# A hybrid mixer layer on one core: the squares of weight blocks kept near their written place on ScalarE, and another order at the output's end

## The chip, the cores and the metric

The kernel runs on one core of one Trainium2 chip. The metric is the device time of one execution in microseconds. A core has five engines with an instruction queue each: TensorE (PE, matmuls; its weight loads are shown as PEld), VectorE (DVE), ScalarE (ACT), GpSimd (POOL) and SyncE (SP), which here only issues DMA transfers. ScalarE and GpSimd issue some transfers too.

## The reference

One layer of a flow-matching backbone, for two groups of tokens, 2048 sample tokens and 128 prompt tokens, with weights shared between them:

```python
xn = rmsnorm(h, ln_g) * (1.0 + scale) + shift          # shift, scale, gate from the conditioning
proj = xn @ w_in                                       # 1024 -> 7696 columns, split by branch
o_a = delta_bidir(...)  * silu(z_a)                    # A: gated delta rule, both directions
o_b = chunk_sgu(u_b, v_b, ...) * silu(z_b)             # B: spatial gating in chunks of 128
o_c = fourier_mix(x_c, grid) * silu(z_c)               # C: real part of an FFT over the grid
merged = sum_n sigmoid(gates[n]) * (o_n @ w_branch[n]) # three branches, 512 -> 1024
h = h + gate * (merged @ w_out)                        # 1024 -> 1024
y = rmsnorm(h, final_g)
```

The outputs are y for the prompt, y for the sample, and the final states of the prompt's delta rule. Everything is in float32; the kernel makes each float32 product of three fp16 matmuls, from a high and a low half of both operands.

## The kernel before, in words

**Stages.** The normalized input is held transposed as fp16 halves (xh, xl: 128 partitions, 8 blocks of 128 channels, 2176 tokens). Tokens are taken in blocks of 512, the last (the prompt) of 128 (TBS). In order of time the kernel computes the silu of z_a, the delta branch's q, k and v (to 440 us in the profile), the spatial gating (to about 745), the Fourier branch (to about 1030), three merges (branch B from about 1030, then C, then A to about 1980), and the output projection with the residual and the last norm (to the end). Since about 440 the delta branch runs beside this as a generator: `pace.tick` and `pace.part` take steps of it by the TensorE time that has been written, first preparation (prep, base_inverse), then from about 890 the scan over chunks, which is a long serial chain of small matmuls.

**Weight blocks.** The input projection and the branch projections are cut into blocks of 128 columns. `read_w` (L291, through `load`) loads a block into a staging buffer `wst`; there are two of these. `converting` (L301 to L328) turns it into halves in steps, each ended by a `yield`: the square (L315, on ScalarE, which writes its squares to the block's low half `lo` as scrap and sums them into `ss`); then a cast of the sum on VectorE (L264), a one-column matmul that adds it over the partitions (`scales`), and a few one-column VectorE instructions for a power-of-two scale; then the high half on ScalarE (L327) and the low half on VectorE (L328), which frees the staging buffer. Large blocks are 128x1024 (`wlo`, `whi`), branch blocks 128x512 (`blo`, `bhi`). `weight_step` takes one such step; `getw(2, 2)` takes the next two blocks and lets the two behind them be converted while these two are used.

In the Fourier stage a loop over four column groups calls `pace.tick` after each part of the work, and every tick takes one weight step. In `merge` (L1699 for the halves of a branch, L1733 for the gate's sigmoid, L1742 and L1743 for the product and the sum) each of eight output blocks goes over five token blocks; behind the gate's and the branch's products of one token block stand a `weight_step()` and a `pace.tick`, so two weight steps. The square of the next gate block is therefore written in the first token block and its one-column matmul directly behind it; the high half and the square of the next branch block are written in the second. At the join of Fourier and the first merge, `branch_block` loads the gated branch from DRAM (`st<-br`, L1689) and makes its halves `big` (o16).

**What sets the order.** The program is written in one order and the Tile scheduler reorders it at compile time: on each engine it issues what it expects to be ready first, with the written order as priority. `tc.issue_after(x)` puts an edge to x on each instruction of a block that goes to x's engine: not before x in the queue, without a wait on the chip. `_InTurn` wraps an engine: with `kept` set, its instructions stay in written order (so at the end of the output: `in_order(True)` for VectorE, ScalarE and TensorE, not for GpSimd); its method `queued()` gives an edge to the engine's newest instruction. `behind_gate()` ties squares and halves to the latest gate sigmoid, but only from the end of the second merge on. Until then a square may be issued as soon as its load is expected.

**The output's end.** The output runs over eight pairs of 128-token row blocks. For the last pair `two_tiles(..., end=True)` and then `prompt_right` write by hand the last products (Y, Z and the prompt's two), the gated residual sums (`add_gated`), the squares for the norm in two or three parts (`squared`), their sums (`summed_up`), the root on GpSimd (`root`), the product with the final gain (`final`), the scaling by the norm (`scaled`) and the stores.

Of the kernel before, what the change touches and what calls it, by code (L numbers as in the profile page):

```python
# [2 lines left out]

# [1 line left out]

# [9 lines left out]
AF = mybir.ActivationFunctionType  # L15
ALU = mybir.AluOpType
# [4 lines left out]
P = 128  # L21
D = 1024
# [7 lines left out]
EPS = 1e-6  # L30
# [138 lines left out]
class _InTurn:  # L169
# [14 lines left out]

        return call

    def queued(self):

        e = self.engine.engine
        newest = next((i for i in reversed(self.tc.nc.cur_bb.bb.instructions) if i.engine == e), None)  # L190
        return ExitStack() if newest is None else self.tc.issue_after(newest)


# [1 line left out]
def hybrid_flow_kernel(ctx: ExitStack, tc: tile.TileContext, x_prompt, x_sample, state_delta, c, c_ctx, w_ada,  # L195
                       b_ada, w_blk, w_bd, a_log, dt_bias, w_spatial, b_spatial, w_brb, w_outb, final_g, w_adb, cols, x_t, x_tp,
                       consts, consts16, y_prompt, y_sample, new_state, dbg=None):
    nc = tc.nc
    SY = nc.sync
    G, V, A, PE = [_InTurn(tc, e_) for e_ in (nc.gpsimd, nc.vector, nc.scalar, nc.tensor)]  # L200
# [17 lines left out]
    ps_mm = pool(ctx, "ps_mm", 3, space=PSUM)  # L218
# [22 lines left out]
    mhalf = sb(cp, [P, 1], "mhalf")  # L241
    G.memset(mhalf, -0.5)

    newest, gated_, queued = [None], [None], [False]

    def behind_gate():
        return tc.issue_after(gated_[0].ins) if queued[0] else ExitStack()
# [55 lines left out]
    def converting(w, st, nkt, cols=P, hi=None, lo=None, tag="w", bufs=5, nth=0):  # L303

        wpool = bwp[0] if tag == "b" else wp
        if tag == "z":
            hi, lo = [sb(p0p, [P, nkt, cols], n_, F16, bufs=4) for n_ in ("zhi", "zlo")]
        if tag == "v":
            hi, lo = [t[:, vfilled[0]] for t in v4]
            vfilled[0] += 1  # L310
        w.hi = sb(wpool, [P, nkt, cols], tag + "hi", F16, bufs=bufs) if hi is None else hi
        w.lo = sb(wpool, [P, nkt, cols], tag + "lo", F16, bufs=bufs) if lo is None else lo
        ss = sb(wp, [P, 1], "wss", bufs=4) if nth < KT else bsums[:, 3 + nth:4 + nth]
        with behind_gate():
            w.squared = A.activation(w.lo, st, AF.Square, accum_out=ss)  # L315
# [11 lines left out]
        w.made = A.activation(w.hi, st, AF.Copy, scale=s)  # L327
        w.low = V.scalar_tensor_tensor(w.lo, st, s, w.hi, ALU.mult, ALU.subtract)  # L328
# [602 lines left out]
    for ct in range(12):  # L931
        w = getw(1, 2 if ct < 6 else min(4, 15 - ct))
        for half in range(1):
# [545 lines left out]
    ps = bank(ps_x, [P, 4, P])  # L1479
# [27 lines left out]
    for t in range(NCH):  # L1507
        ps = bank(ps_mm, [P, 4, P])
# [34 lines left out]
    for g in range(4):  # L1543
# [14 lines left out]
    vst.close()  # L1558


    fs = ExitStack()
    fp = pool(fs, "fp", 1)
    for n_, (a, b) in _COFF.items():
# [14 lines left out]
    for g in range(4):  # L1578
        xw, zw = getw(2, 2)
        for gh in range(1):  # L1580
# [68 lines left out]
            for q4 in range(5):  # L1649
# [8 lines left out]
                if q4 == 2:  # L1658
                    ps = bank(ps_x, [P, P])
# [129 lines left out]
    gates = gate_rows()  # L1789
    s1_, inv_ = branch_scale(1, 20)  # L1790
    inv_ = merge(1, True, inv_, then=(2, 20))
    def finish_delta(db):
        if db == KT - 1:
            pace.drain()
            queued[0] = True
# [97 lines left out]
    ps = bank(ps_x, [P, 27])  # L1893
# [13 lines left out]
    p16, gp, last_load = [], [], []  # L1907
# [36 lines left out]
    wo = _W()  # L1944
# [33 lines left out]
    nth = [0]  # L1978
# [31 lines left out]
    def two_tiles(t, pa, xr, hh, end):  # L2010
# [47 lines left out]
        product(Y, pa, 2, summed(3), False)  # L2058
        Z = bank(ps_mm, [P, 512])
        product(Z, pa, 6, quarter(4, 512), True)  # L2060
        final(hh[0], hh[0], left, left, V)
        final(hh[1], hh[1], right, right, G)
        summed_up(1, 0)
        summed_up(0, 0)
        add_gated(hh[1][:, left], Y, gb[:, left], p1, V)
        squared(1, 1, xr[1], hh[1], left)
        final(hh[1], hh[1], left, left, G)
        add_gated(hh[0][:, right], Z, gb[:, right], u2, V)
        squared(0, 1, xr[0], hh[0], right)
# [7 lines left out]
    def scaled(j, t):  # L2077
        h = last_rows[j]
        A.activation(h, h, AF.Copy, scale=norms[:, j:j + 1])
        SY.dma_start(y_sample[0, (t + j) * P:(t + j + 1) * P], h)  # L2080

    def in_order(kept):
        V.kept = A.kept = PE.kept = kept
# [1 line left out]
    last_rows = []  # L2085
# [3 lines left out]
    def squared(j, i, junk, h, cs):  # L2089
        A.activation(junk[:, cs], h[:, cs], AF.Square, accum_out=parts[j][:, i:i + 1])  # L2090

    def final(out, h, cs, fs, on):
        on.tensor_tensor(out[:, cs], h[:, cs], fg[:, fs], ALU.mult)

    def summed_up(j, i):
        q_ = parts[j]
        if i:
            V.scalar_tensor_tensor(q_[:, i:i + 1], q_[:, i:i + 1], 1.0 / D, q_[:, i - 1:i], ALU.mult, ALU.add)
        else:
            V.tensor_scalar(q_[:, 0:1], q_[:, 0:1], 1.0 / D, EPS, ALU.mult, ALU.add)  # L2100

    def root(j, i):
        G.tensor_tensor(norms[:, j:j + 1], parts[j][:, i:i + 1], mhalf, ALU.pow)
# [12 lines left out]

    def prompt_right():
        cols = slice(0, 384), slice(384, 512)
        summed_up(2, 0)
        for i, cs in enumerate(cols):  # L2120
            ps = bank(ps_mm, [P, cs.stop - cs.start])
            gemm_N(ps, *p16, wo, 512 + cs.start, cs.stop - cs.start)
            add_gated(gp_right[:, cs], ps, gp_right[:, cs], x_right[:, cs], V)
            squared(2, 1 + i, x_right, gp_right, cs)
        scaled(0, firsts[-1])
        f_ = room[:, (2 - 2 * nth[0]) * D:(2 - 2 * nth[0]) * D + 512]
        for cs in cols:
# [7 lines left out]
        SY.dma_start(y_prompt[0, :, right], f_)  # L2135

    in_turn(x_left, xp_[0:P, left])
    next_pair(in_turn)
# [52 lines left out]
```

## Time and profile before

| | us |
|---|---|
| median of three runs | 2145.2 |
| the runs | 2149.37, 2145.2, 2144.76 |
| profiled execution | 2150.07 |
| its span, from the first to the last instruction | 2148.3 |
| TensorE busy in the span | 2085.2 |
| DMA | 403.25 MB, mean 188 GB/s |

The profiled execution is one of its own, 4.87 us above the median of the runs. Times of instructions are counted from the start of its span. A row of a timeline gives start, duration, engine, line, operation and tiles, and in brackets how long the engine was idle before and what released it; x12 is twelve instructions drawn together. A row of the squares and halves reads `wlo<-wst` for a large block and `blo<-wst` for a branch block. In a row of windows stand the stretch, its length, the busy time of PE, PEld, DVE, ACT and POOL with their instructions, the granted TensorE clock as a share of full speed, the DMA engines' busy share and GB/s. In the rows of the output's end, L182 is the wrapper's own line, since instructions in kept order are recorded there.

### The profile page before, as it was taken

The page shows a single profiled execution, that of the slowest core. Times are in us where ns is not written, and L with a number is a line of the kernel's source. Part 1 is how long each engine was busy: PE and PEld are TensorE (multiplying, and loading weights), DVE is VectorE, ACT ScalarE, POOL GpSimd, SP SyncE. Part 2 cuts the span into 40 slices and gives each one's busy share as a digit, 9 for nine tenths or more (in the row PEclk, how much of TensorE's full clock was granted, in tenths as well). Part 3 has the DMA queues.
Part 4 walks back from the last instruction along what each step waited for, and adds up shares of the span by engine and source line. Part 5 has one row for each costly group of instructions (what it writes and reads, how often), then busy time and mean ns, then how long its engine had stood idle before and what let it go on. Part 6 is the DMA issues. An engine that isn't in the chain of part 4 may idle for free.

```text
span 2148.3 us, 42630 instructions
## 1 busy us (share of the span) xinstructions
PE 2085.2 (97%) x16133; PEld 1196.8 (56%) x16133; DVE 1327.9 (62%) x2945; ACT 1060.8 (49%) x2457; POOL 843.3 (39%) x1089
## 2 busy tenths in 40 slices
PE   7999999999999999989899999999999999999997
PEld 4454444455555677777555556565655444444443
DVE  6656854388777786456655555766665564666245
ACT  5554744475656664445544445665653353453112
POOL 0321332225565555542321233354542234333464
PEclk9999999999999999999999999999999999999999
DMA  9525722277877743444655555867664655456852
GB/s 353 219 77 189 267 102 102 74 223 226 259 228 246 225 138 93 121 132 138 205 182 161 167 162 184 258 206 232 210 204 127 209 167 173 167 198 240 335 220 89
DMA packets 222910, 403.25 MB, mean 188 GB/s; under 512 B 39720, under 2 KB 109632, under 8 KB 219888
## 3 DMA queue, kind: packets, MB, share of 16 engines
q1 hardware_dynamic: 167664, 290.84, 42.5%
q0 software_dynamic: 15216, 65.89, 8.2%
q10 hardware_dynamic: 39824, 43.79, 6.0%
q8 instruction: 127, 2.08, 0.4%
q14 instruction: 79, 0.65, 0.1%
HBM read 258.19 MB, written 142.24 MB: 186 GB/s over the span
## 4 chain that ended last, share of the span: by engine, by line
PE 70%; DVE 9%; DMA 9%; ACT 4%; POOL 4%; issue 3%; SPq 1%; ACTq 0%; DVEq 0%; POOLq 0%
PE b L250 66%; PE b L182 4%; DMA st<-br 2%; POOL E L1115 1%; DMA pa<-pa 1%; DMA wst<-in_w_blk_dram 1%; DVE XB L1114 1%; POOL st L1466 1%; DMA ab<-in_w_adb_dram 1%; PE b L1016 1%; DMA sqk<-qk 1%; DMA ei<-XB 0%; ACT xh L182 0%; ACT nd L1066 0%; DVE XB L1123 0%
## 5 line engine op out<-in xcount | busy, mean ns | idle before, releaser
L250 PE MATMUL b<-xh,whi 128*128 128x512 f16 (+1 forms) x1920 | 651.1, 348 | 2.8 <-DVE sg L1456 1.8
L250 PE MATMUL b<-xl,whi 128*128 128x512 f16 (+1 forms) x1920 | 651.2, 348 | 0.0
L250 PE MATMUL b<-xh,wlo 128*128 128x512 f16 (+1 forms) x1920 | 650.1, 347 | 0.0
L250 PEld LDWEIGHTS <-whi 128*128 128x128 f16 x3856 | 352.7, 98 | 326.4 <-issue 7.3
L250 PEld LDWEIGHTS <-wlo 128*128 128x128 f16 x1928 | 188.8, 98 | 176.1 <-issue 2.2
L250 PE MATMUL b<-big,bhi 128*128 128x512 f16 (+1 forms) x960 | 252.3, 347 | 1.9 <-ACT big L1699 1.1
L250 PE MATMUL b<-big,blo 128*128 128x512 f16 (+1 forms) x480 | 163.1, 347 | 0.0
L1743 POOL TENSOR_TENSOR mrow<-mrow,sg 128x512 f32<-128x512 f32 (+1 forms) x80 | 94.4, 1182 | 131.2 <-DVE sg L1742 99.5
L953 POOL TENSOR_TENSOR cy<-cy,raw 128x545 f32<-128x545 f32 (+1 forms) x48 | 65.8, 1395 | 181.8 <-ACT raw L952 181.8
L250 PEld LDWEIGHTS <-xh 128*128 128x128 f16 x1496 | 116.9, 98 | 28.8 <-issue 1.4
L250 PEld LDWEIGHTS <-bhi 128*128 128x128 f16 x960 | 87.7, 98 | 78.1 <-issue 2.6
L1115 POOL TENSOR_TENSOR E<-E,XB 128x31 f32<-128x31 f32 (+15 forms) x155 | 94.1, 607 | 85.7 <-DVE XB L1114 68.8
L250 PEld LDWEIGHTS <-xl 128*128 128x128 f16 x1068 | 98.1, 98 | 44.8 <-DMA tw<-tw 1.4
L1733 ACT ACTIVATE sg<-b,winv 128x512 f32<-128x512 f32 (+1 forms) x120 | 73.9, 616 | 87.1 <-PE b L250 86.4
L1188 POOL COPY T<-ES 32x256 f16<-32x256 f16 x68 | 31.8, 467 | 188.6 <-DMA ES<-ei 167.9
L250 PE MATMUL b<-whi,xh 128*128 128x128 f16 x544 | 92.8, 219 | 0.0
L250 PE MATMUL b<-whi,xl 128*128 128x128 f16 x544 | 92.8, 219 | 0.0
L250 PE MATMUL b<-wlo,xh 128*128 128x128 f16 x544 | 92.8, 219 | 0.0
L328 DVE SCALAR_TENSOR_TENSOR wlo<-wst,wsc,whi 128x1024 f16<-128x1024 f32 x52 | 71.1, 1368 | 33.1 <-ACT whi L327 32.7
L315 ACT ACTIVATE wlo<-wst 128x1024 f16<-128x1024 f32 x52 | 54.9, 1055 | 54.5 <-DMA wst<-in_w_blk_dram 51.2
L1114 DVE TENSOR_TENSOR XB<-XB,E 128x31 f32<-128x31 f32 (+15 forms) x155 | 55.2, 356 | 41.8 <-POOL E L1115 41.2
L1295 POOL TENSOR_TENSOR skn<-skn,ed 128x512 f32<-128x512 f32 x34 | 37.7, 1109 | 109.7 <-DMA skn<-kv 109.7
(532 smaller groups left out, 4317.9 us busy)
## 6 DMA issues: line engine op xcount, KB each, us to landing
wst<-in_w_blk_dram SPq DMA_DIRECT2D x58, 512.0 KB, 4.5
pa<-pa POOLq DMA_DIRECT2D x16, 896.0 KB, 4.4
qkv<-cy POOLq DMA_DIRECT2D x12, 1089.0 KB, 5.3
st<-br SPq DMA_DIRECT2D x48, 256.0 KB, 3.2
mrow<-mrg SPq DMA_DIRECT2D x16, 576.0 KB, 4.6
pa<-pa SPq DMA_DIRECT2D x5, 1792.0 KB, 17.3
dc<-dec SPq DMA_DIRECT2D x17, 512.0 KB, 4.8
kq<-qkv SPq DMA_DIRECT2D x34, 256.0 KB, 4.5
```

Source lines behind the costliest of these rows:

```text
L182: self.last = f(*args, **kw)
L250: newest[0] = PE.matmul(out, l, r, start=start, stop=stop, skip_group_check=reopened)
L315: w.squared = A.activation(w.lo, st, AF.Square, accum_out=ss)
L328: w.low = V.scalar_tensor_tensor(w.lo, st, s, w.hi, ALU.mult, ALU.subtract)
L953: G.tensor_tensor(y[:, c0:c1], y[:, c0:c1], raw[:, 1 + c0:1 + c1], ALU.mult)
L1016: PE.transpose(ps[:, hs(h)], cur[part][:, h, :], ident)
L1114: V.tensor_tensor(t3, X3[:, 0:k, k:k + 1].to_broadcast([P, k, n_]), E3[:, k:k + 1, k:32].to_broadcast([P, k, n_]), ALU.mult)
L1115: G.tensor_tensor(E3[:, 0:k, k:32], E3[:, 0:k, k:32], t3, ALU.subtract)
L1188: G.tensor_copy(T16[rows(a0, b), :, :, b], ES[0:32, :, 2 * a0 + b, :, wT])
L1295: G.tensor_tensor(h3(kn_), h3(kn_), bc(ed[:, d, t, :], P), ALU.mult)
L1733: gated_[0] = A.activation(sg, ps, AF.Sigmoid, scale=gw.inv)
L1743: G.tensor_tensor(mr, mr, sg, ALU.add)
```

## The change

Two edits. First, `queued` takes a number n and gives an edge to the n-th newest instruction of its engine; while the list `scanning` is not empty, from the start of the Fourier stage to the end of the first merge, a weight block's square has an edge to the twelfth newest ScalarE instruction written so far. Loads, halves and sums are not touched.

Second, the hand-written end. VectorE's product of row block 0's left half with the gain (`final(hh[0], left)`) and the first small sums move behind the two last gated sums; GpSimd's left half of row block 1 is written last, and VectorE keeps the right half of row block 0, now in `prompt_right`. The small sums are turned round: the first adds D times epsilon, and only the last multiplies by 1/D. `prompt_right` writes both of its products first, weaves row block 0's sums and root into its own, and lets ScalarE do the prompt's squares before it scales row block 1 and then row block 0. Row block 0's store goes through ScalarE's queue. The prompt's output is put together in one 128x1024 buffer by VectorE, where ScalarE had scaled the left half, and leaves in one store of 512 KB instead of two of 256 KB.

```diff
-    def queued(self):
+    def queued(self, n=1):
         e = self.engine.engine
-        newest = next((i for i in reversed(self.tc.nc.cur_bb.bb.instructions) if i.engine == e), None)
+        own = (i for i in reversed(self.tc.nc.cur_bb.bb.instructions) if i.engine == e)
+        newest = next(islice(own, n - 1, None), None)
         return ExitStack() if newest is None else self.tc.issue_after(newest)
...
-        with behind_gate():
+        with behind_gate(), A.queued(12) if scanning else ExitStack():
             w.squared = A.activation(w.lo, st, AF.Square, accum_out=ss)
...
+    scanning.append(True)
     fs = ExitStack()
...
     inv_ = merge(1, True, inv_, then=(2, 20))
+    scanning.clear()
...
-        final(hh[0], hh[0], left, left, V)
-        final(hh[1], hh[1], right, right, G)
-        summed_up(1, 0)
-        summed_up(0, 0)
         add_gated(hh[1][:, left], Y, gb[:, left], p1, V)
         squared(1, 1, xr[1], hh[1], left)
-        final(hh[1], hh[1], left, left, G)
+        final(hh[1], hh[1], right, right, G)
         add_gated(hh[0][:, right], Z, gb[:, right], u2, V)
         squared(0, 1, xr[0], hh[0], right)
-        summed_up(1, 1)
+        final(hh[0], hh[0], left, left, V)
+        summed_up(1, 0)
+        summed_up(1, 1, True)
         root(1, 1)
-        final(hh[0], hh[0], right, right, V)
-        summed_up(0, 1)
-        root(0, 1)
-        scaled(1, t)
+        final(hh[1], hh[1], left, left, G)
...
-        summed_up(2, 0)
-        for i, cs in enumerate(cols):
-            ps = bank(ps_mm, [P, cs.stop - cs.start])
-            gemm_N(ps, *p16, wo, 512 + cs.start, cs.stop - cs.start)
-            add_gated(gp_right[:, cs], ps, gp_right[:, cs], x_right[:, cs], V)
-            squared(2, 1 + i, x_right, gp_right, cs)
-        scaled(0, firsts[-1])
-        f_ = room[:, (2 - 2 * nth[0]) * D:(2 - 2 * nth[0]) * D + 512]
-        for cs in cols:
-            final(f_, gp_right, cs, slice(512 + cs.start, 512 + cs.stop), V)
+        end = []
+        for cs in cols:
+            end.append(bank(ps_mm, [P, cs.stop - cs.start]))
+            gemm_N(end[-1], *p16, wo, 512 + cs.start, cs.stop - cs.start)
+        V.tensor_tensor(gp_right[:, cols[0]], end[0], gp_right[:, cols[0]], ALU.mult)
+        summed_up(0, 0)
+        summed_up(0, 1, True)
+        root(0, 1)
+        V.tensor_tensor(gp_right[:, cols[0]], gp_right[:, cols[0]], x_right[:, cols[0]], ALU.add)
+        squared(2, 1, x_right, gp_right, cols[0])
+        add_gated(gp_right[:, cols[1]], end[1], gp_right[:, cols[1]], x_right[:, cols[1]], V)
+        squared(2, 2, x_right, gp_right, cols[1])
+        scaled(1, firsts[-1], SY)
+        final(last_rows[0], last_rows[0], right, right, V)
+        summed_up(2, 0)
         summed_up(2, 1)
-        summed_up(2, 2)
+        summed_up(2, 2, True)
         root(2, 2)
-        A.activation(x_left, x_left, AF.Copy, scale=norms[:, 2:3])
-        A.dma_start(y_prompt[0, :, left], x_left)
-        V.tensor_scalar(f_, f_, norms[:, 2:3], None, ALU.mult)
-        SY.dma_start(y_prompt[0, :, right], f_)
+        out = room[:, (2 - 2 * nth[0]) * D:(3 - 2 * nth[0]) * D]
+        V.tensor_tensor(out[:, right], gp_right, fg[:, right], ALU.mult)
+        scaled(0, firsts[-1], A)
+        V.tensor_scalar(out[:, left], x_left, norms[:, 2:3], None, ALU.mult)
+        V.tensor_scalar(out[:, right], out[:, right], norms[:, 2:3], None, ALU.mult)
+        SY.dma_start(y_prompt[0], out)
```

More of the change, by code (lines that the diff above doesn't have):

```diff
@@ L2 @@
 from contextlib import ExitStack
+from itertools import islice
 import numpy as np
@@ L242, in hybrid_flow_kernel @@
     G.memset(mhalf, -0.5)
-    newest, gated_, queued = [None], [None], [False]
+    newest, gated_, queued, scanning = [None], [None], [False], []
     def behind_gate():
@@ L2060, in two_tiles, with scaled @@
         product(Z, pa, 6, quarter(4, 512), True)
-        final(hh[0], hh[0], left, left, V)
-        final(hh[1], hh[1], right, right, G)
-        summed_up(1, 0)
-        summed_up(0, 0)
         add_gated(hh[1][:, left], Y, gb[:, left], p1, V)
         squared(1, 1, xr[1], hh[1], left)
-        final(hh[1], hh[1], left, left, G)
+        final(hh[1], hh[1], right, right, G)
         add_gated(hh[0][:, right], Z, gb[:, right], u2, V)
         squared(0, 1, xr[0], hh[0], right)
-        summed_up(1, 1)
+        final(hh[0], hh[0], left, left, V)
+        summed_up(1, 0)
+        summed_up(1, 1, True)
         root(1, 1)
-        final(hh[0], hh[0], right, right, V)
-        summed_up(0, 1)
-        root(0, 1)
-        scaled(1, t)
-    def scaled(j, t):
+        final(hh[1], hh[1], left, left, G)
+    def scaled(j, t, queue):
         h = last_rows[j]
         A.activation(h, h, AF.Copy, scale=norms[:, j:j + 1])
-        SY.dma_start(y_sample[0, (t + j) * P:(t + j + 1) * P], h)
+        queue.dma_start(y_sample[0, (t + j) * P:(t + j + 1) * P], h)
     def in_order(kept):
@@ L2093, in final, with summed_up @@
         on.tensor_tensor(out[:, cs], h[:, cs], fg[:, fs], ALU.mult)
-    def summed_up(j, i):
+    def summed_up(j, i, whole=False):
         q_ = parts[j]
         if i:
-            V.scalar_tensor_tensor(q_[:, i:i + 1], q_[:, i:i + 1], 1.0 / D, q_[:, i - 1:i], ALU.mult, ALU.add)
+            V.tensor_scalar(q_[:, i:i + 1], q_[:, i:i + 1], q_[:, i - 1:i], 1.0 / D if whole else 1.0, ALU.add, ALU.mult)
         else:
-            V.tensor_scalar(q_[:, 0:1], q_[:, 0:1], 1.0 / D, EPS, ALU.mult, ALU.add)
+            V.tensor_scalar(q_[:, 0:1], q_[:, 0:1], D * EPS, None, ALU.add)
     def root(j, i):
```

## The prediction

> **What bounds the kernel now.** I read the page first, then the windows by stage, the waits, the timelines around the long gaps, and the end.
>
> ```profile
> span 2148.3 us, 42630 instructions
> PE 2085.2 (97%) x16133; PEld 1196.8 (56%) x16133; DVE 1327.9 (62%) x2945; ACT 1060.8 (49%) x2457; POOL 843.3 (39%) x1089
> L315 ACT ACTIVATE wlo<-wst 128x1024 f16<-128x1024 f32 x52 | 54.9, 1055 | 54.5 <-DMA wst<-in_w_blk_dram 51.2
> ```
>
> TensorE is busy for 2085.2 of 2148.3 us, so 63 us of idleness and whatever a lower clock costs are all that an order of instructions can win. The squares of the weight blocks (L315) look like a large item, since ScalarE idles 54.5 us before the 52 large ones, 51.2 of it until a weight load has landed. ScalarE is only 49% busy, though, so this counts only where TensorE waits behind it. The windows, split by stage, show where TensorE waits at all; the columns are the stretch, its length, busy time of PE, PEld, DVE, ACT and POOL, the granted clock and the DMA share.
>
> ```profile
> 745.00:890.00 145.00, 139.89 (x1855) 115.17 (x1853) 103.88 (x254) 77.61 (x198) 74.79 (x119) 0.99 0.40 122
> 890.00:945.00 55.00, 45.87 (x516) 32.70 (x514) 27.36 (x67) 22.49 (x58) 25.41 (x45) 0.91 0.49 140
> 945.00:1020.00 75.00, 73.53 (x1112) 61.90 (x1111) 48.80 (x129) 38.00 (x96) 28.41 (x45) 1.00 0.47 139
> 1020.00:1085.00 65.00, 57.14 (x462) 33.79 (x460) 43.80 (x110) 37.44 (x82) 19.92 (x25) 0.92 0.67 208
> 1085.00:1355.00 270.00, 269.57 (x2450) 160.69 (x2449) 153.74 (x408) 129.71 (x310) 79.74 (x122) 1.00 0.56 171
> 1700.00:1980.00 280.00, 278.92 (x1548) 135.82 (x1547) 166.72 (x371) 123.05 (x209) 106.73 (x117) 1.00 0.55 186
> ```
>
> The Fourier stage (745 to about 1030) loses 5.1, 9.1 and 1.5 us, the join of Fourier and first merge (1020 to 1085) 7.9, and the rest of the first merge only 0.4 us in 270. So the 15 us or so of squares' waits in the merge proper are free; what the first edit can win sits before 1085.
>
> **The change, part by part: the squares.** The edit adds no instruction. It ties the squares of these blocks, told by their high halves from 735 to 1380, to an order edge:
>
> ```profile
> L327 ACT ACTIVATE whi<-wst,wsc x15: 1132/1148/1165, 759.7 to 1348.9; 128x1024 f16<-128x1024 f32 x15
> L327 ACT ACTIVATE bhi<-wst,wsc x9: 705/721/722, 1027.9 to 1373.5; 128x512 f16<-128x512 f32 x9
> ```
>
> Each of the 24 is then issued at most twelve ScalarE instructions ahead of where the code writes it. Now they run far ahead:
>
> ```profile
> 1100.40 1.06 ACT L315 ACTIVATE wlo<-wst 128x1024 f16<-128x1024 f32 x1 [2.24 <-DMA wst<-in_w_blk_dram]
> 1134.59 1.15 ACT L327 ACTIVATE whi<-wst,wsc 128x1024 f16<-128x1024 f32 x1
> ```
>
> These belong to one block: the square stands 34 us ahead of the high half that needs its sum, holds ScalarE's in-order queue for 2.24 us until the load lands, and gains nothing, because the sum's one-column matmul keeps its written place on TensorE. After the edit such a square comes at most some 10 us early (310 instructions in 270 us, 0.87 us each, times 12), long after its load. VectorE's cast of the sum moves with it. The staging buffer is released by the low half, which doesn't move, so SP's loads and what is queued behind them stay too. The square's own 1.06 and 0.19 us fall elsewhere on a half-idle engine: cost nothing, and if that cover were gone, 24 times about 1.1 us on ScalarE.
>
> One place of the four above carries a gain that I can trace:
>
> ```profile
> 1030.38 0.51 PE L250 MATMUL b<-T,sn 128*128 128x64 f16 x12
> 1030.49 0.63 ACT L1231 ACTIVATE S<-S 128x512 f16<-128x512 f32 x1 [1.37 <-DVE S L1345]
> 1032.65 0.63 ACT L315 ACTIVATE blo<-wst 128x512 f16<-128x512 f32 x1 [1.52 <-DMA wst<-in_w_brb_dram]
> 1033.28 0.67 ACT L1733 ACTIVATE sg<-b,winv 128x512 f32<-128x512 f32 x1
> 1033.97 0.38 ACT L1218 ACTIVATE Q<-b 64x256 f16<-64x256 f32 x1
> 1034.96 0.68 PE L250 MATMUL b<-R,Q 128*128 128x64 f16 x12 [1.72 <-DVE Q L1219]
> 1051.58 0.67 ACT L1733 ACTIVATE sg<-b,winv 128x512 f32<-128x512 f32 x1
> ```
>
> The matmuls into Q's bank are over at 1030.9. ScalarE could take the gate's sigmoid and then Q from 1031.1, but its next instruction is the square of the first merge's second branch block, which waits 1.52 us for its load and then works 0.63. Q comes at 1033.97 instead of about 1031.8, VectorE's half follows, and TensorE stands 1.72 us. The code writes that square behind the second token block's sigmoid, which runs at 1051.58; the timeline has more than twenty ScalarE instructions between, so twelve do not bring it back to here. Step one: **-1.7 us**.
>
> The gap has a follower:
>
> ```profile
> 1031.70:1035.14 3.44, 1.12 (x25) 1.05 (x25) 1.69 (x8) 2.44 (x7) 3.22 (x4) 1.00 1.01 356
> 1035.14:1038.55 3.41, 2.14 (x27) 1.93 (x24) 2.45 (x9) 3.33 (x10) 0.00 (x0) 0.50 0.66 197
> 1038.55:1041.97 3.42, 2.76 (x30) 2.49 (x29) 2.88 (x8) 1.24 (x3) 0.00 (x0) 0.50 0.80 239
> 1041.97:1045.38 3.41, 3.41 (x23) 1.73 (x21) 2.32 (x5) 2.55 (x9) 0.84 (x1) 0.50 0.98 248
> ```
>
> After 3.44 us with only 1.12 busy, the granted clock is half for the next 10.2 us. TensorE's work there, 2.14 + 2.76 + 3.41 = 8.3 us, would have taken half as long: 4.2 us lost. Whether this goes depends on what is left in the stretch: 0.7 of its 2.3 idle us remain. The section "Part 1: The HAM clock gate" of the Trainium skill's page "TensorE: Matmul & The Clock Gate" says that the clock halves after an idle window of about 3.4 us. By that rule read strictly the stretch above, a third busy, would not have cost the clock, and closing the gap would return 1.7 us and no more; the row shows the half clock all the same.
>
> A third place is the square of the next gate block, ahead of the loading of o16 (L1699, L1700):
>
> ```profile
> 1049.91 1.06 ACT L315 ACTIVATE wlo<-wst 128x1024 f16<-128x1024 f32 x1 [1.77 <-DMA wst<-in_w_blk_dram]
> 1054.03 0.38 PE L250 MATMUL b<-big,bhi 128*128 128x512 f16 x1 [0.39 <-ACT big L1699]
> ```
>
> It holds ScalarE for 2.8 us; TensorE waits 0.39 us for o16 just after. **-0.4 us**; the later waits there follow st's loads, with the DMA share at 0.67 over 1020 to 1085, and I count no more. In Fourier the largest waits of TensorE are for loads of the scan:
>
> ```profile
> PE b L250 <- DMA ES<-ei: 3.6, 2, 2.5
> PE b L250 <- DMA N<-n: 1.9, 1, 1.9
> ```
>
> They do not depend on the squares, so I count nothing. The changed order could move that stage by a gap like these, about 2 us either way; that is my bound from both sides.
>
> **The end.** The reordering takes VectorE's product of row 0 and two small sums from ahead of the last two pairs, adds one-column sums later, moves the two sample rows' scaling behind the prompt's squares on ScalarE, gives one row's store to ScalarE's queue, and writes the prompt's output in one 512 KB store instead of two of 256 KB. ScalarE's 0.6 us on x_left goes to VectorE (0.49).
>
> ```profile
> 2131.09 0.69 DVE L182 TENSOR_TENSOR xh<-xh 128x512 f32<-128x512 f32 x1
> 2134.48 0.67 DVE L182 TENSOR_TENSOR xh<-b,wst 128x512 f32<-128x512 f32 x1
> 2136.71 1.69 POOL L2093 TENSOR_TENSOR xh<-xh,fg 128x512 f32<-128x512 f32 x1 [2.83 <-ACT xh L182]
> 2137.20 1.23 DVE L182 SCALAR_TENSOR_TENSOR part<-part 128x1 f32<-128x1 f32 x1
> 2139.46 1.15 ACT L182 ACTIVATE xh<-xh,norms 128x1024 f32<-128x1024 f32 x1 [1.43 <-POOL norms L2103]
> 2140.64 2.17 SPq L2080 DMA_DIRECT2D out_dram<-xh  x2
> 2142.92 0.36 SPq L2135 DMA_DIRECT2D out_dram<-xh  x1
> 2143.16 0.38 ACTq L182 DMA_DIRECT2D out_dram<-xh  x1
> ```
>
> VectorE now starts Y's pair at 2131.8 instead of 2134.48. Not all of this survives: the one-column sum of 2137.20 ended with POOL's product (2138.40), so the two exclude each other. I lay the new order out with 0.69 us per VectorE product (0.55 where it has waited) and 1.27 to 1.7 on POOL: Y's pair to 2133.2; POOL's right product to 2134.5; Z's pair to 2135.0; POOL's left product to 2136.3; row 0's left product to 2136.8; sums 2137.05; root of row 1 2137.6. The prompt's products with the sums between end at 2139.0, its squares at 2139.5, row 1's scaling at 2140.6 (its store issued as now, 2140.64), row 0's at 2141.7, the prompt's row at 2141.8. So the last issue comes at about 2142.1 instead of 2143.16, 1.0 us earlier. The stores, however, fill the queues:
>
> ```profile
> 2141.00:2142.00 1.00, 0.00 (x0) 0.00 (x0) 0.64 (x4) 1.00 (x5) 0.18 (x1) 0.53 0.56 225
> 2142.00:2143.00 1.00, 0.00 (x0) 0.00 (x0) 0.49 (x1) 1.00 (x2) 0.37 (x1) 0.50 0.74 299
> 2144.00:2145.00 1.00, 0.00 (x0) 0.00 (x0) 0.00 (x0) 0.00 (x0) 0.00 (x0) 0.50 0.97 381
> 2145.00:2146.00 1.00, 0.00 (x0) 0.00 (x0) 0.00 (x0) 0.00 (x0) 0.00 (x0) 0.50 1.01 373
> ```
>
> At the end the DMA share is 1. All three stores hold 1.57 MB either way. With the last two present from about 2142.65, some 0.42 MB is through by then and 1.15 MB at 377 GB/s takes 3.05 us: 2145.7 instead of 2146.05. **-0.4 us** (bounds: -1.5 if row 1's store also comes earlier, +0.6 if POOL's left product delays the first root by half of its 1.27 us).
>
> **The sum.** Against the profiled execution (2150.07 us; span 2148.3 and 1.8 around it): -1.7 - 0.4 - 0.4 = -2.5, and -4.2 more where the half clock goes: 2147.6 or 2143.4. That execution was 4.9 us over the median of the runs, 2145.2, about the price of that half clock. So I take it that the median runs mostly did not pay it; then the edit cannot return it there, and I predict 2145.2 - 2.5 = **2142.7 us**.
>
> **The rivals.**
> *The half clock is in the median too.* Then it goes as well: 2142.7 - 4.2 = 2138.5. For it: the stretch's 1.12 busy us come from the kernel's own order. Against: the 4.9 us between the profile and the median.
> *The wait is replaced.* The freed ScalarE slots fill with the gate blocks' squares, now written near the join, and Q comes late anyway; only the end's 0.4 is left: 2144.8. For it: of the 7.9 idle us there I can give only 2.1 to squares, and the DMA share is 1.01 from 1031.7.
> *Slower: the sum comes too late for TensorE.* In a merge token block a gate block's square and its one-column matmul are written directly behind each other, so TensorE meets that matmul right behind the branch product. If the square did run at its written place, TensorE would stand for 1.06 + 0.19, about 0.15 for the cast and some 0.2 between them, 1.6 us. Over the 8 gate blocks of the merge this is 13 us, 2155.5; a third of them, 2147. It decides once fewer than 1.6 us of ScalarE's twelve instructions lie ahead; 10 us are typical, but a backlog on ScalarE eats them. With a half clock behind two or three such gaps (3.4 us at half clock, 1.7 each) my figure is 2151. Against it: the window of 1700 to 1980, where the code already ties these squares to the latest sigmoid, idles 1.1 us in 280.
>
> **How the numbers follow.** Forecast 0.44, its own range 2140 to 2145; half clock gone too 0.27; replaced 0.13; slower 0.16. A measurement of this kernel tells about 0.2% (4.3 us) from no change, so faster means under 2140.9: the second case and a third of the first, 0.42; slower, over 2149.5, is the last case's 0.16 whole; the rest 0.42. The range leaves out a tenth on either side: 2136.5 to 2150.
>
> **What would show it.** In the changed profile no square between 745 and 1380 waits for wst; from 1020 to 1085 TensorE idles under 6 us; the clock stays 1.00 near 1035; the merge still idles under 1 us; the last store is issued about 1 us earlier after the last matmul and the last byte 0.4 us earlier. I am wrong if TensorE waits for wscb's casts, if Fourier loses more than now, or if the stores at the end run one behind another.

## The result and the profile after

| | before | after |
|---|---|---|
| median, us (10 runs each, on one chip) | 2144.98 | 2154.53 |
| lowest and highest | 2142.19, 2151.39 | 2150.07, 2159.05 |
| profiled execution | 2150.07 | 2155.36 |
| its span | 2148.3 | 2153.3 |
| last matmul ends | 2136.2 | 2143.1 |

The ratio is 1.0035, 95% interval 1.0023 to 1.0047: slower by about 7.5 us, where 2142.7 was forecast. A row of the page after:

```profile
PE 2086.8 (97%) x16133; PEld 1198.4 (56%) x16133; DVE 1330.9 (62%) x2945; ACT 1059.0 (49%) x2456; POOL 840.8 (39%) x1089
```

TensorE has the same 16133 matmuls and 1.6 us more busy time; its last matmul ends 6.9 us later, so the other 5.3 us are waiting. The windows of after, by the stages that the prediction used (stretch, its length, busy time of PE, PEld, DVE, ACT, POOL, granted clock, DMA share, GB/s):

```profile
745.00:890.00 145.00, 136.47 (x1763) 111.04 (x1761) 102.75 (x251) 75.50 (x196) 80.98 (x127) 0.98 0.43 132
890.00:945.00 55.00, 48.19 (x647) 38.34 (x645) 34.37 (x83) 26.56 (x69) 20.88 (x41) 0.94 0.43 124
945.00:1020.00 75.00, 74.00 (x1073) 61.12 (x1072) 46.47 (x118) 35.03 (x90) 26.96 (x44) 1.00 0.42 131
1020.00:1085.00 65.00, 56.09 (x506) 34.49 (x503) 46.37 (x116) 39.96 (x88) 24.71 (x33) 0.95 0.67 217
1085.00:1355.00 270.00, 269.96 (x2438) 160.49 (x2436) 152.30 (x401) 127.01 (x309) 74.39 (x114) 1.00 0.55 170
```

Fourier (745 to 1020) idles 8.5 + 6.8 + 1.0 = 16.3 us (before 15.7), the join 8.9 (7.9), the first merge 0.04 (0.4). All that the edit touches is within about a microsecond of before. (A single execution tells no more at the join: e5 below, whose queues up to there are those of before, idles 10.0 us in it, e9 7.3.) Most of the loss stands behind it, in the first part of the second merge, where no square is tied. There, first before, then after:

```profile
1355.00:1400.00 45.00, 42.12 (x375) 24.81 (x373) 32.19 (x79) 28.70 (x76) 16.80 (x20) 1.00 0.83 270
1400.00:1430.00 30.00, 30.00 (x294) 18.76 (x293) 18.51 (x49) 18.66 (x55) 14.38 (x18) 1.00 0.67 199
```

```profile
1355.00:1400.00 45.00, 41.31 (x357) 24.17 (x356) 31.67 (x81) 30.24 (x80) 13.33 (x19) 1.00 0.86 263
1400.00:1430.00 30.00, 26.67 (x238) 16.14 (x236) 18.70 (x44) 15.36 (x43) 14.78 (x18) 0.94 0.61 203
```

Before, TensorE idles 2.9 us in these 75, all ahead of 1400; after, 3.7 + 3.3 = 7.0, and the clock is lower. The longest gap, in the timeline of after:

```profile
1417.80 1.27 POOL L1746 TENSOR_TENSOR mrow<-mrow,sg 128x512 f32<-128x512 f32 x1 [0.55 <-POOL R L1192]
1418.01 1.07 DVE L327 TENSOR_TENSOR winv<-wsc,xsc 128x1 f32<-128x1 f32 x1
1419.26 1.15 POOL L1300 TENSOR_TENSOR kn<-skn,kn 128x512 f16<-128x512 f32 x1 [0.19 <-ACT kn L1299]
1419.31 1.12 DVE L1712 TENSOR_TENSOR binv<-binv,xsc 128x1 f32<-128x1 f32 x1
1420.35 0.74 DVE L330 SCALAR_TENSOR_TENSOR blo<-wst,wsc,bhi 128x512 f16<-128x512 f32 x1
1421.01 1.11 DVE L1347 SCALAR_TENSOR_TENSOR S<-S,egl,b 128x128 f32<-128x128 f32 x4
1422.84 0.22 PE L252 MATMUL b<-S,sk 128*128 128x128 f16 x1 [2.67 <-ACT S L1233]
```

Read it from the bottom. TensorE's matmul S,sk, a step of the scan, waits 2.67 us for ScalarE's half of S, which waits for VectorE's update of the state (L1347). That update stands in VectorE's queue behind the conversion of a weight block: two one-column products (1.07 and 1.12 us for 128 numbers) and the low half. The same scan step before:

```profile
1413.93 0.24 DVE L325 TENSOR_TENSOR winv<-wsc,xsc 128x1 f32<-128x1 f32 x1
1416.63 0.16 DVE L1709 TENSOR_TENSOR binv<-binv,xsc 128x1 f32<-128x1 f32 x1
1417.73 1.12 DVE L1345 SCALAR_TENSOR_TENSOR S<-S,egl,b 128x128 f32<-128x128 f32 x4 [0.61 <-PE b L250]
1421.43 0.22 PE L250 MATMUL b<-S,sk 128*128 128x128 f16 x1
```

Here a block's conversion was over before the state was due; VectorE even stood idle 0.61 us, and S,sk found its operand without a wait. Neither instruction was edited. After the gap the clock goes too (windows of after around it):

```profile
1419.70:1423.20 3.50, 0.83 (x10) 0.46 (x8) 3.47 (x8) 0.96 (x2) 0.71 (x1) 1.00 0.22 75
1423.20:1426.60 3.40, 3.40 (x25) 2.42 (x23) 1.64 (x6) 2.49 (x8) 0.00 (x0) 0.51 0.74 230
```

A stretch with 0.83 of 3.50 us busy is followed by 3.4 us at half clock, worth 1.7 us. With the 4.1 us more of waiting these are 5.8 of the 6.9 us.

### The profile page after: what moved, and what is told of

It reads as the page before. It is cut to its first block, busy times and chain, and to the rows that moved or that the text cites. A ratio compares the mean times of both kernels' runs of the same rounds, so it can differ in the third digit from the quotient of the medians.

```text
span 2153.3 us, 42643 instructions
## 1 busy us (share of the span) xinstructions
PE 2086.8 (97%) x16133; PEld 1198.4 (56%) x16133; DVE 1330.9 (62%) x2945; ACT 1059.0 (49%) x2456; POOL 840.8 (39%) x1089
## 4 chain that ended last, share of the span: by engine, by line
PE 52%; DVE 7%; DMA 6%; POOL 3%; ACT 3%; issue 3%; SPq 1%; ACTq 0%; POOLq 0%; DVEq 0%
PE b L252 52%; DMA st<-br 1%; POOL E L1117 1%; DMA pa<-pa 1%; DVE XB L1116 1%; POOL st L1468 1%; DVE XB L1125 0%; ACT big L1702 0%; DMA wst<-in_w_blk_dram 0%; ACT nd L1068 0%; DMA ES<-ei 0%; DMA ei<-XB 0%; POOL ss L1026 0%; DMA sq__1371_11667<-qT 0%; DVE sg L1458 0%
## 5 line engine op out<-in xcount | busy, mean ns | idle before, releaser
L1745 DVE SCALAR_TENSOR_TENSOR sg<-b,binv,sg 128x512 f32<-128x512 f32 (+1 forms) x80 | 53.4, 668 | 41.2 <-PE b L252 35.8
```

What stands on the lines that cost most here:

```text
L1745: V.scalar_tensor_tensor(sg, ps, binv[:, 1:2], sg, ALU.mult, ALU.mult)
```

## The experiments

Sixteen kernels. Theory A: the edges make the Tile scheduler order the second merge otherwise, and that order costs. Rival B: the squares' sums come late and TensorE waits for their one-column matmul (the prediction's slower case). Rival C: the new end costs. Orders are compared in the built queues, where the kernels' instructions can be told one by one.

**Splitting the change (e1 to e4).** The squares' edit without the new end; the new end without the squares' edit; then the ties kept to one stage, with the end as before:

In e3:

```diff
-    inv_ = merge(1, True, inv_, then=(2, 20))
-    scanning.clear()
+    scanning.clear(); inv_ = merge(1, True, inv_, then=(2, 20))
```

In e4:

```diff
-    scanning.append(True)
...
-    inv_ = merge(1, True, inv_, then=(2, 20))
+    scanning.append(True); inv_ = merge(1, True, inv_, then=(2, 20))
```

> The squares' order edge as in the change, the output's end as before. Theory A (the edge makes the scheduler put the delta branch's instructions in another order, and TensorE loses at the new order's waits): slower than before by 8 to 10 us, since the whole change lost about 7.5 and the changed profile's end, from the last matmul to the end of the span, is 2 us shorter; the extra idle time and half clock lie from 1385 to 1460 and at single gaps before 1085, and no matmul waits for a square's sum. Theory B (the squares' sums come too late for their one-column matmul in the merge): the same 8 to 10 us, but TensorE's idle time between 1085 and 1355 grows from 0.4 us to several. Theory C (the new end costs the time): within 2 us of before.

> The output's end as in the change, the squares free as before. Theories A and B: faster than before by 1 to 2 us, all of it behind the last matmul (from 12.1 us there to about 10.1). Theory C: slower by 5 us or more.

> The squares' edge only from the start of the Fourier stage to just before the first merge; end as before. Theory A: the loss is not bound to the number of squares tied. It comes with the order in which the second merge and the scan's chunks meet, so this kernel has either nearly none of it (under 2 us) or nearly all (6 to 10). Theory B: no loss, within 2 us, since a Fourier tick lies between a square and its sum's matmul.

> The squares' edge only in the first merge; end as before. Theory A: as for the Fourier part, nearly none or nearly all of the loss; together the two need not add up to the whole. Theory B: the whole loss, 8 to 10 us, with TensorE idle between 1085 and 1355 for several us.

Measured, as the ratio to before: e1 1.0026 (1.0016 to 1.0037), e2 0.9988 (0.998 to 0.9996), e3 0.9998 (0.9988 to 1.0009), e4 1.0036 (1.0022 to 1.0049). C falls: the end gains. e1 lost 5.6 us (3.4 to 7.9), less than the 8 to 10 expected of theory A. The ties in Fourier cost nothing that the interval can tell; those in the first merge cost as much as the whole change. From 1355 to 1460 TensorE idles 6.7 us in e1 and 7.0 in e4, but 4.0 in e2 and 1.5 in e3.

**One square (e5, e6).** The first merge's last tied square belongs to the second merge's first branch block (`nth == 16`): 0.6 us of work. e5 ties it alone, with the old end; e6 is the whole change with only this square left free.

In e5, then in e6:

```diff
-        with behind_gate(), A.queued(12) if scanning else ExitStack():
+        with behind_gate(), A.queued(12) if scanning and nth == 16 else ExitStack():
```

```diff
-        with behind_gate(), A.queued(12) if scanning else ExitStack():
+        with behind_gate(), A.queued(12) if scanning and nth != 16 else ExitStack():
```

> One single square is tied, that of the second merge's first branch block (0.6 us, written in the last output block of the first merge); all others are free and the end is as before. In the built queues every engine then has the order of the kernel before up to that square and the order of the changed kernel behind it, and the second merge's scan matmuls stand on average 17 to 19 large matmuls earlier in TensorE's queue. Theory A (the order of the second merge carries the loss, and it comes from where the scheduler puts the scan's matmuls): slower than before by 5 to 8 us, with 6 to 9 us of idle time and half clock from 1355 to 1460 where before has 2.9. Theory B (many squares late by themselves): within 1 us of before.

> The whole change, new end too, with that one square left free: 23 of the 24 stay tied. The second merge's queues are those of the kernel before. Theory A: faster than before by 1 to 4 us (the new end's 2 to 3 us), so 9 to 11 us faster than the change. Theory B: slower than before by 4 us or more.

Measured: e5 1.0033 (1.0019 to 1.0048), e6 0.9994 (0.9983 to 1.0005). One order edge on one instruction carries the loss. The windows of e5:

```profile
1355.00:1400.00 45.00, 42.11 (x370) 24.63 (x368) 32.00 (x78) 30.96 (x81) 11.13 (x13) 1.00 0.83 261
1400.00:1430.00 30.00, 25.11 (x225) 14.89 (x224) 19.97 (x46) 15.48 (x44) 15.16 (x21) 1.00 0.65 199
```

It idles 2.9 + 4.9 us, the place of after's loss; against before that is 4.9 of its about 7.1 us. In the built queues the square stands 19 places later on ScalarE than before, and behind it 2532 of TensorE's 31626 matmuls and weight loads stand elsewhere; the scan's small matmuls come on average 17 to 19 large matmuls earlier.

**Other numbers in the merge (e7, e8).** The first merge's squares, and no others, tied with 24 or with 6 in place of 12, with the old end:

```diff
-        with behind_gate(), A.queued(12) if scanning else ExitStack():
+        with behind_gate(), A.queued(24) if scanning else ExitStack():
```

> The first merge's 17 squares tied to the twenty-fourth newest ScalarE instruction in place of the twelfth, end as before. The built order of TensorE in the second merge is nearly that of the kernel before. Theory A: within 2 us of before. Theory B: a loss smaller than at twelve but there, 3 to 6 us.

> The same with the sixth newest: squares closer to their place than in the change. In the built queue the second merge's scan matmuls stand 5 to 48 large matmuls later than before, not earlier. Theory A: no loss from 1355 to 1460 (idle time and half clock at most the 2.9 us of before), the whole within 2 us of before or faster, unless the later scan adds a wait where the second merge ends. Theory B: more than the loss at twelve, 8 us or more.

Measured: e7 0.9991 (0.998 to 1.0003); e8 1.0063 (1.0048 to 1.0079). e7, whose second merge is nearly in the old order, is level as expected. e8 was a miss of theory A as I then held it: its scan stands later, not earlier, and it lost twice as much. From 1355 to 1460 it idles 5.7 us, but most of its waits lie further on; the row of its windows has 8.6 us idle where before has 1.9, and a row of its timeline shows one of the gaps:

```profile
1460.00:1700.00 240.00, 231.36 (x1881) 133.66 (x1880) 134.02 (x332) 117.06 (x338) 99.39 (x115) 0.99 0.59 184
```

```profile
1507.24 0.98 PE L252 MATMUL b<-u,sqk 128*128 128x128 f16 x12 [3.03 <-ACT o L1243]
```

So "earlier" is not what costs; another order meets other gaps.

**The late square against the order (e9), and the whole change with other numbers (e10 to e12).** Of the numbers that I built for the one square alone (4, 8, 10, 11, 13, 14, 16, 20, 24 and 12), only 12 gives another second merge. With 4 the square itself stands even later than with 12.

In e9, then in e10 (e11 and e12 have 11 and 8 there):

```diff
-        with behind_gate(), A.queued(12) if scanning and nth == 16 else ExitStack():
+        with behind_gate(), A.queued(4) if scanning and nth == 16 else ExitStack():
```

```diff
-        with behind_gate(), A.queued(12) if scanning else ExitStack():
+        with behind_gate(), A.queued(14) if scanning else ExitStack():
```

> The one square (second merge, first branch block) tied with 4 instead of 12, the rest as before. In the built queues it then stands 33 places later on ScalarE than before, where 12 put it 19 places later, and yet TensorE's order behind the join stays that of before but for 35 of its 31626 matmuls and loads (12: 2532). Theory A (the loss is the other order of the scan's matmuls in the second merge): ratio to before 0.999 to 1.001, and 1355 to 1460 idles 2 to 4 us as before. Rival B (the late square itself, or the sum behind it, makes TensorE wait): at least the 1.0033 of the tie with 12, with the idle time at that square.

> The whole change with 14 in place of 12, new end and all. Second merge in the order of before; Fourier in another. Theory A: the end's gain alone is left, ratio 0.9980 to 0.9995, and 1355 to 1460 idles 2 to 4 us. If the number 12 is nothing special and holding the squares costs by itself: 1.0035 as the change.

> The whole change with 11 in place of 12. The second merge gets an order of its own: the scan's matmuls stand on average 8.6 and then 3.7 large matmuls earlier than before, about half of what 12 does. If the loss follows the distance (A1): about half of the change's, ratio 1.000 to 1.002. If it hangs on single meetings of a scan step with a weight conversion on VectorE's queue (A2): anything from 0.998 to 1.004, with the idle time in gaps of 1 to 3 us behind one-column work, not spread. Rival B: 1.0035.

> The whole change with 8 in place of 12. The scan's matmuls stand 5 to 12 large matmuls later in the second merge's first half and where they were in the rest. A1 (only an earlier scan loses in proportion): 0.998 to 0.999. A2 (any other order meets other gaps; the tie with 6 in the first merge, later by 5 to 48, lost 13 us): 1.000 to 1.005, with gaps of 1 to 3 us between 1380 and 1700. Rival B: above 1.0035, since the squares come later still.

Measured: e9 0.9993 (0.9981 to 1.0005), e10 0.9992 (0.9982 to 1.0002), e11 1.0028 (1.0018 to 1.0039), e12 1.0018 (1.0006 to 1.003). The windows of e9:

```profile
1355.00:1400.00 45.00, 41.43 (x360) 23.92 (x359) 32.80 (x79) 30.98 (x83) 18.03 (x23) 1.00 0.80 259
1400.00:1430.00 30.00, 30.00 (x293) 19.15 (x292) 18.05 (x49) 15.76 (x47) 13.19 (x18) 1.00 0.72 220
```

A square tied more tightly costs nothing that the interval can tell if the order behind it stays: B falls, and A is shown. In e11 most of the idle time sits elsewhere than I expected, at the join (11.9 us, before 7.9); two rows of its timeline:

```profile
1036.13 0.63 ACT L317 ACTIVATE blo<-wst 128x512 f16<-128x512 f32 x1 [5.84 <-DMA wst<-in_w_brb_dram]
1038.00 0.26 PE L252 MATMUL b<-S,sk 128*128 128x128 f16 x1 [6.50 <-ACT S L1233]
```

With 11 the square that the edit was to hold back stands ahead of the scan's S on ScalarE and waits 5.84 us for its load: the very wait that the prediction saw removed, several times as long. And e12, whose ties end with the first merge, meets the same at a free gate square of the second:

```profile
1590.70 1.06 ACT L317 ACTIVATE wlo<-wst 128x1024 f16<-128x1024 f32 x1 [4.01 <-DMA wst<-in_w_blk_dram]
1592.42 0.22 PE L252 MATMUL b<-u,kn 128*128 128x128 f16 x1 [2.10 <-ACT u L1233]
```

So A1 (loss in proportion to the distance) falls by e8 and e12. A2 (single meetings) agrees with these gaps, though they do not stand only behind one-column work as I had put it; how much of each loss such gaps make was not counted.

**What is in the gap (e13, e14).** In after's longest gap the two one-column products end where GpSimd's product beside them ends: 1418.01 + 1.07 = 1419.08 against 1417.80 + 1.27 = 1419.07, then 1420.43 against 1420.41. The Trainium skill's page "SBUF — State Buffer", section "Who interferes with whom", says that a VectorE instruction with two inputs in SBUF and a GpSimd instruction that reads SBUF exclude each other. If a per-partition scalar does not count as an input there, it frees the product. e13 does this to the order of e5, e14 to the kernel before; in both the order behind the join stays nearly the same.

```diff
-            V.tensor_mul(w.inv, inv, isx)
+            V.tensor_scalar(w.inv, inv, isx, None, ALU.mult) if merging else V.tensor_mul(w.inv, inv, isx)
...
-            V.tensor_mul(binv[:, 0:1], inv, bw.inv)
-            V.tensor_mul(binv[:, 1:2], binv[:, 0:1], sx)
+            V.tensor_scalar(binv[:, 0:1], inv, bw.inv, None, ALU.mult)
+            V.tensor_scalar(binv[:, 1:2], binv[:, 0:1], sx, None, ALU.mult)
```

> The losing order of the one tied square, with the one-column products of the merges (the weight's scale and the two of the branch's) written as a product with a per-partition scalar instead of one of two tensors; in the built queues the second merge's order stays the losing one. Theory P (in the 2.12 us gap ahead of S,sk at 1425.98 VectorE's two products of 1.07 and 1.12 us waited for GpSimd's product beside them, because both operands were tensors): they take 0.15 to 0.3 us, the gap falls to about 0.3 (2.12 - 2 x 0.95), 1400 to 1430 idles 2 to 3 us instead of 4.9, and the ratio to before falls from 1.0033 to 1.0020 to 1.0026. Rival Q (they waited for something else, an operand or the queue itself): their length, the gap and 1.0033 stay.

> The kernel before with the same three products by a per-partition scalar, its order behind the join nearly kept. P: only what these products hold in the good order comes back, where no gap over 1 us stands behind them: 0.9985 to 1.0005. If e13 gains no more than this one does, the gap was not what cost. Q: 1.000.

Measured, on one chip: e13 1.0011 (1.0001 to 1.0021), e14 0.9981 (0.997 to 0.9993). The same step in e13:

```profile
1420.07 1.27 POOL L1747 TENSOR_TENSOR mrow<-mrow,sg 128x512 f32<-128x512 f32 x1 [0.54 <-POOL R L1193]
1420.28 0.21 DVE L328 TENSOR_SCALAR winv<-wsc,xsc 128x1 f32<-128x1 f32 x1
1420.78 0.21 DVE L1713 TENSOR_SCALAR binv<-binv,xsc 128x1 f32<-128x1 f32 x1
1423.63 0.22 PE L253 MATMUL b<-S,sk 128*128 128x128 f16 x1 [1.33 <-ACT S L1234]
```

The products take 0.21 us beside a running GpSimd product, so the page's rule agrees here, and theory P is right about their length. Its two ranges, 1.0020 to 1.0026 and 0.9985 to 1.0005, were both missed on the fast side. But the gap shrank by 0.8 us (2.12 to 1.33), not by 1.9, and e14 gained 0.0019 where no such gap stood, about as much as e13 did against e5 (0.0022). What I had put down as the test, that e13 gains no more than e14, came out against the gap: e13 is still 0.0030 behind e14, and the loss of that order is as large as ever. Its windows, then e14's:

```profile
1355.00:1400.00 45.00, 41.34 (x367) 24.34 (x366) 32.12 (x76) 30.23 (x80) 10.89 (x13) 1.00 0.85 262
1400.00:1430.00 30.00, 27.23 (x267) 16.93 (x267) 18.60 (x49) 16.69 (x46) 16.14 (x22) 1.00 0.70 218
```

```profile
1355.00:1400.00 45.00, 42.56 (x382) 25.23 (x380) 33.23 (x81) 29.73 (x78) 15.99 (x20) 1.00 0.86 276
1400.00:1430.00 30.00, 30.00 (x294) 18.75 (x293) 18.56 (x48) 18.26 (x53) 14.86 (x18) 1.00 0.66 200
```

6.4 us idle against 2.4: the order's loss is spread over several waits of the scan, and with one shortened the others remain.

**Putting the gains together (e15, e16).** e15 is the whole change with 14 and the products by a scalar; e16 the new end and those products, with no square tied.

> The whole change with 14 in place of 12 and the three products by a per-partition scalar. Sum of what each measured alone: the ties at 14 with the new end 0.9992, and 0 to -0.001 for the products: 0.998 to 0.9995.

> No square tied; the new end, and the merges' one-column products by a per-partition scalar. If the two gains lie in different places they add up: 0.9988 x 0.9981 = 0.9969, range 0.996 to 0.998. If squares tied at 14 had been worth something, it would be no better than the 0.9989 measured with them.

Measured: e15 0.9989 (0.998 to 0.9999), e16 0.9991 (0.9978 to 1.0003). The two gains, 0.9988 and 0.9981, did not add up to 0.9969; e16's own interval leaves out that sum. The lowest of the sixteen ratios is e14's, 0.19% with an interval of 0.07 to 0.3%. That gain is not confirmed: with the same products e15 is level with e10 (0.9989, 0.9992) and e16 with e2 (0.9991, 0.9988).

## Why the prediction was wrong, point by point

- **The step that failed** is the price of the order: "The changed order could move that stage by a gap like these, about 2 us either way; that is my bound from both sides." It was given to Fourier alone, and the part behind the first merge, where no square is tied, stood at nothing; "SP's loads and what is queued behind them stay too" is the same error. A tied instruction shifts what the scheduler places after it, without limit to the tied stage. e5 and e9 show it: the same square, tied at 12 costs 0.33%, about 7 us, tied at 4 nothing that the interval can tell. The prediction's range had no case for it: its slower rival had the sign right and the mechanism wrong. No matmul of the first merge waited for a sum; the merge idles 0.04 us.
- **The wait at 1033 (-1.7): moved, and replaced.** The timeline of after at that place:

```profile
1032.09 1.04 ACT L317 ACTIVATE wlo<-wst 128x1024 f16<-128x1024 f32 x1
1033.37 0.77 PE L252 MATMUL b<-S,sk 128*128 128x128 f16 x11 [0.85 <-DVE S L1234]
1033.83 0.38 ACT L1220 ACTIVATE Q<-b 64x256 f16<-64x256 f32 x1
1034.23 1.14 ACT L1243 ACTIVATE o<-b,eg 128x128 f32<-128x128 f32 x4
1034.72 0.51 PE L252 MATMUL b<-R,Q 128*128 128x64 f16 x12 [0.36 <-DVE Q L1221]
1035.25 0.64 ACT L317 ACTIVATE blo<-wst 128x512 f16<-128x512 f32 x1
1066.24 0.45 PE L252 MATMUL b<-ES,N 128*128 128x32 f16 x8 [2.45 <-DMA ES<-ei]
```

  The branch block's square (`blo`) stands behind Q now, and TensorE waits 0.36 us for Q's half where it waited 1.72. But a gate block's square (`wlo`) has taken its slot: Q still comes 2.6 us after the matmuls into its bank (before 3.1). TensorE waits about 0.8 us at a time for other steps of the scan, and 2.45 us later for a load; the join idles 8.9 us, not under 6. That is the rival "the wait is replaced", as it was described. Timed, e6 and e10 (squares tied, old order in the second merge, new end; 0.9994 and 0.9992) are no better than the new end alone (0.9988): apart from the order, the ties are worth nothing that the intervals can tell.
- **"At most twelve ScalarE instructions ahead" did not hold.** The edge counts in the written order, and the scheduler also moves the instruction at its other end. The branch block's square is written behind a sigmoid that runs at 1049.48. In the built queue its edge leads to the last o of the row at 1034.23, which the scheduler has moved 21 places ahead of that sigmoid, and the square follows it at once. With 11 (e11) it even stands ahead of S.
- **The half clock (-4.2, not counted): shortened, not gone.** Windows of after:

```profile
1034.10:1037.50 3.40, 1.81 (x35) 1.41 (x32) 3.03 (x14) 3.38 (x11) 1.81 (x4) 1.00 0.98 351
1037.50:1040.90 3.40, 2.46 (x29) 2.57 (x30) 3.04 (x8) 2.20 (x7) 0.00 (x0) 0.51 0.77 195
1040.90:1044.30 3.40, 2.83 (x22) 1.57 (x20) 2.41 (x7) 2.40 (x6) 0.00 (x0) 0.50 0.77 230
```

  It costs half of 2.46 + 2.83, 2.6 us. The reason for leaving it out, that the profiled execution alone paid it, was weak: the profiles of before, of after and of all sixteen kernels show half clock between 1020 and 1085, and single runs of before, on one chip, from 2142.19 to 2151.39 show that 4.9 us between one execution and a median of three runs is no evidence. The Trainium skill's page "TensorE: Matmul & The Clock Gate", section "Part 1: The HAM clock gate", has the clock halved after an idle window. Here a stretch 53% busy and, at 1419.70, one 24% busy came ahead of it, so, the page read strictly, the measurement differs.
- **The gate square at 1050 (-0.4)** can't be told in so changed a join: from 1020 to 1085 TensorE waits 1.5 us for o16 in all, before 1.8. **Fourier (0, within 2)** was right: 16.3 us idle against 15.7, and e3 at 0.9998.
- **The first merge** was right: still under 1 us idle, and no tied square waits for its load. One square between 745 and 1380 does (at 1358.38, 2.4 us); it is a free one of the second merge.
- **The end (-0.4): right in sign, too small.** Rows of after's timeline; then windows of the stores, two of before and one of after:

```profile
2142.91 0.22 PE L183 MATMUL b<-wohi,wlo 128*128 128x128 f16 x1
...
2147.13 0.33 SPq L2079 DMA_DIRECT2D out_dram<-xh  x1
2148.17 0.38 ACTq L183 DMA_DIRECT2D out_dram<-xh  x1
2148.88 0.33 SPq L2141 DMA_DIRECT2D out_dram<-xh  x1
```

```profile
2141.43:2142.75 1.32, 0.00 (x0) 0.00 (x0) 0.55 (x3) 1.32 (x2) 0.55 (x1) 0.50 0.98 397
2142.75:2143.25 0.50, 0.00 (x0) 0.00 (x0) 0.14 (x1) 0.38 (x1) 0.00 (x0) 0.50 0.01 0
```

```profile
2147.93:2151.85 3.92, 0.00 (x0) 0.00 (x0) 0.88 (x2) 0.21 (x1) 0.01 (x1) 0.50 1.01 401
```

  The last issue comes 5.75 us after the last matmul (before 2143.16 - 2136.20 = 6.96): 1.2 earlier, where 1.0 was laid out. The last byte came about 1.1 us earlier (8.7 after the last matmul; before 9.85) and not 0.4. The term that was mis-sized is the stores' time. The 225 and 299 GB/s of the prediction's rows are means over whole microseconds, and these hold stretches without a transfer; the first old store ran at 397 GB/s while it ran, and then 0.5 us passed before the next one's bytes. In after the three follow each other without a gap, and the first begins 4.8 us after the last matmul instead of 5.2. From the last matmul to the span's end it is 10.1 to 10.6 us in the eight profiles with the new end (mean 10.3) and 11.6 to 12.1 in the ten with the old one (mean 11.8): -1.6, by the timed runs of e2 -2.6 (-0.9 to -4.3). The lower bound of that step, -1.5, was the better figure.

What stays open: that the order costs is shown, and one gap was followed to its instructions, but why just the tie at 12 flips the scheduler, and which of the scan's waits make up the 0.3%, were not separated: in e5 about 2 of about 7 us stand outside the windows shown.

## What to carry to other kernels

Where a scheduler orders the program, a tie on one instruction is a change to everything behind it: compare the built queues with the old ones before pricing the tie, and price a changed stage by what other orders cost (here 0 to 0.6%), even if no line of it was edited. Try the neighbours of a hand-chosen number: here 14 and 24 left the later order alone, while 8, 11 and 12 lost 0.2 to 0.35%, and 6, in the merge alone, 0.6%. An edge to the n-th newest instruction holds a place only as far as that instruction stays in its own. A wait taken away gains only what the next wait in line leaves; read the follower's slack first.

## What was not expected of the hardware

- A 128x1 product of two tensors on VectorE takes 0.16 us undisturbed and as long as the GpSimd product beside it (1.07 and 1.12 us); by a per-partition scalar it takes 0.21 us beside one. From 1085 to 1980 the 44 such products of the weights' scale have a mean of 302 ns before and 211 in e14 (rows of the groups by line; total us, then mean ns):

```profile
L325 DVE TENSOR_TENSOR winv<-wsc,xsc 128x1 f32<-128x1 f32 x44 | 13.3, 302 | 1.1
```

```profile
L326 DVE TENSOR_SCALAR winv<-wsc,xsc 128x1 f32<-128x1 f32 x44 | 9.3, 211 | 1.2
```

- One store of 512 KB alone moved 397 GB/s with the DMA share at 0.98 (before, 2141.43 to 2142.75); three on two queues moved no more, 401 GB/s (after). What differed was the gap between them.
